# Attention tail of a two-layer encoder: masks as identity matmuls, two O/den pairs in the last units, 1/den products on GpSimd

## The chip, the cores and the metric

The kernel is one program that runs on all 8 cores of one Trainium2 chip; each core does one of the 8 sequences of the batch. The metric is the device time of the slowest core in microseconds. Most executions agree within 0.3%. Some fall in a second, slower state, in which the cores of one die (four cores) show a lower granted TensorE clock and the run is longer. "Ratio" is always the mean time of one kernel's fast runs over the mean of the other's fast runs of the same rounds, so it is not quite the ratio of the medians that are quoted beside it.

Engine names in the profile: PE is TensorE, DVE is VectorE, ACT is ScalarE, POOL is GpSimd, SP is SyncE (SPq: its queue of DMA issues).

## The reference, cut to what matters

Only layer 0's attention is touched by the change. There are 15 heads of 64 columns in three groups with dilations 1, 4 and 16, over 2048 tokens.

```python
q = rope(rms_norm(q, q_norm), pos); k = rope(rms_norm(k, k_norm), pos)
for g in range(3):                       # dilations 1, 4, 16; five heads each
    s = where(valid, q k^T * 64**-0.5, NEG_INF)      # a band of keys per query
    p = exp(s - max(s)); den = sum(p); o = (p / den) v; lse = m + log(den)
wts = softmax(stack(lses), axis=0)       # over the three groups
o = concatenate([outs[g] * wts[g]]) ; x = x + o @ w_o
# then norm, feed-forward, layer 1 (gated short convolution), feed-forward, norm
```

With those weights each group's output is its unnormalised sum of p v, divided by the sum of the three groups' denominators. The kernel uses that: it adds up the denominators of three units and multiplies each unit's output by 1/den at the end.

## The kernel before: the parts that the change and the argument touch

Attention is cut into eight units. Units 0 to 2 are the head pair (0, 1) in groups 0, 1, 2; units 3 to 5 are the pair (2, 3) in the same groups; unit 6 is head slot 4 in groups 1 and 2; unit 7 is head slot 4 in group 0. Units 6 and 7 are the tail. While TensorE does unit u, the projections of later units fill its idle time. A small scheduler orders all operations with cost estimates; each engine then runs its own queue strictly in that order.

The rotary step of a unit (`rope_a`, `rope_b`) multiplies by the cosine and sine tables, adds, and multiplies by norm factors. For that it loads a pair-swapped copy of the data ("arena<-arena" in the DMA views), stores the norm factors to DRAM ("scr<-arena"), and loads them back broadcast over the partitions ("arena<-scr").

```python
def rope_b(u, which, dst, rows=None):                      # cut
    TT("dve", rw, rw, cos_table, ALU.mult)                 # needs the projection
    TT("dve", sw, sw, sin_table, ALU.mult)                 # needs the swapped copy
    TT("dve", rw, rw, sw, ALU.add)
    TT("dve", dst, rw, rbc, ALU.mult)                      # needs the broadcast factors
# unit 7 has its queries in rows 0-63 and its keys in rows 64-127;
# after its last multiply a DMA copies the keys down ("k7")
```

Attention itself: score matmuls, one exponential on ScalarE, a 0/1 mask multiply on VectorE, output (O) and denominator (den) matmuls into one pair of banks of PSUM (the memory that matmuls write), and then an evacuation that adds the denominator into `dtot`:

```python
pO = (6, 7)                                  # the one O/den pair
bo, bd = pO
...
MMS(scores, ...)                             # one key tile after the other
ACT(P, psum, AF.Exp, scale=0.125)
TT("dve", pv, pv, map_, ALU.mult)            # the mask, 0 or 1
out_mms(P, parts)                            # O and den of one block, then evacuate(B_)

def finalize(units, lo, n):                  # 1/den, then one product per unit
    ACT(a, a, AF.Ln); ACT(a, a, AF.Exp, scale=-1.0)
    for u in units:
        TT("dve", o, o, dtot[rows, lo:lo + n], ALU.mult)   # 12 products per three units
```

## Time and profile before

The kernel before takes 1534.3 us (median of three runs, 1533.9 to 1534.9).

| stage | what the profile shows |
|---|---|
| whole span | TensorE busy 1471.2 us, 96% of 1531.6 us; the chain that ended last is 93% TensorE |
| 250 to 325 us (units 6 and 7) | the only long loose stretch; clock 0.50 from 259 to 317 us, but for one window at full clock (266 to 269 us) |
| 255 to 274 us | TensorE waits for unit 6's rotary step |

The page has a view of the span in 40 equal slices of 38.3 us. Each digit of the PE row is the busy share in tenths; each digit of the PEclk row is the granted clock in tenths. These are the two rows of the kernel before:

```profile
PE   5999997699999999999999999999999999999997
PEclk8999999589999999999999999999999999999999
```

The seventh and eighth digits of the PE row (7 and 6, 230 to 306 us) are where TensorE has less work, and the eighth and ninth of the PEclk row (5 and 8) are where its clock is halved: the tail. Apart from the start and the very end, TensorE is full everywhere else.

The timeline of one engine lists its groups of instructions. Columns: start in us, duration in us, engine, line, operation, output and input, shapes, how many; in brackets, the idle time before it and what ended that. First TensorE on core 7, the slowest core:

```profile
253.76 1.59 PE L317 MATMUL psum<-arena 128*128 128x512 bf16 x20 [2.15 <-ACT arena L511]
260.91 5.20 PE L317 MATMUL psum<-arena 128*128 128x512 bf16 x12 [5.56 <-DVE arena L333]
273.97 2.00 PE L317 MATMUL psum<-arena 64*128 64x256 bf16 x8 [7.86 <-DVE arena L333]
276.32 11.38 PE L317 MATMUL psum<-arena 64*128 64x256 bf16 x40 [0.35 <-ACT arena L328]
289.33 2.76 PE L317 MATMUL psum<-arena 128*64 128x256 bf16 x8 [1.63 <-ACT arena L343]
```

Unit 5 ends at 255.4 us. Twelve output-projection matmuls fill part of the wait; unit 6's scores (64 rows) start at 273.97. The 1.63 us at 289.33 is one wait for the single O/den pair. Then the broadcast load's issue on SyncE's queue, and VectorE on the same core:

```profile
253.07 3.14 SPq L349 DMA_DIRECT2D arena<-scr  x2
```

```profile
181.58 7.10 DVE L333 TENSOR_TENSOR arena<-arena 128x2048 bf16<-128x2048 bf16 x6 [0.88 <-DMA arena<-arena]
258.23 7.31 DVE L333 TENSOR_TENSOR arena<-arena 128x512 bf16<-128x512 bf16 x12 [0.94 <-ACT arena L328]
271.47 4.62 DVE L333 TENSOR_TENSOR arena<-arena 128x2048 bf16<-128x2048 bf16 x4 [5.92 <-DMA arena<-scr]
```

The first line is the rotary step ahead of unit 3: six multiplies in 7.10 us, 1.2 us each. The second is the twelve 1/den products of units 3 to 5, 0.6 us each, all done while the broadcast is on its way. The third is the rotary step that the tail waits for: its operand landed at 271.4 us, 18.3 us after its issue.

### The profile page before, as it was taken

Reading aid. Unit: us, or ns where it says so; the run is one execution under the profiler, and the core shown is the slowest. Engines: PE = TensorE matmul, PEld = TensorE weight load, DVE = VectorE, ACT = ScalarE, POOL = GpSimd, SP = SyncE. Lnnn points to the kernel's source line nnn. Section 1 sums busy time; section 2 is a strip of 40 time slices with the busy share of each in tenths; the row PEclk is TensorE's granted clock in tenths of the full one; section 3 lists DMA queues with packets and bytes.
Section 4 is the critical chain, followed back from the end, with each engine's and each line's share of the span. In section 5 each row is a group of like instructions: output and inputs, shape, how many; then the busy total and the mean of one; then the engine's idle time right before and its main releaser. Section 6 shows DMA issues by size and latency. Waiting matters only on the chain.

```text
span 1531.6 us, 19902 instructions; the slowest of 8 cores (1524.7 to 1531.6 us)
## 1 busy us (share of the span) xinstructions
PE 1471.2 (96%) x7312; PEld 684.8 (45%) x7312; DVE 576.6 (38%) x820; ACT 490.7 (32%) x777; POOL 380.3 (25%) x387
## 2 busy tenths in 40 slices
PE   5999997699999999999999999999999999999997
PEld 2656443243344444444444444444444444444445
DVE  4646677556114013013036444456123023032047
ACT  3566686343320220310334333333310310301333
POOL 5100000100350540630620223210530621612600
PEclk8999999589999999999999999999999999999999
DMA  9944445630330420410410433310410411312014
GB/s 252 186 86 100 86 114 110 186 76 1 55 56 1 70 42 0 83 28 2 75 22 1 62 42 49 56 28 7 76 28 3 81 28 24 60 28 49 8 55 166
DMA packets 60910, 95.00 MB, mean 62 GB/s; under 512 B 3792, under 2 KB 40912, under 8 KB 58768
## 3 DMA queue, kind: packets, MB, share of 16 engines
q0 software_dynamic: 52016, 69.18, 25.9%
q1 hardware_dynamic: 8800, 24.55, 5.2%
q8 instruction: 61, 1.00, 0.3%
q14 instruction: 33, 0.27, 0.1%
HBM read 127.37 MB, written 8.52 MB: 89 GB/s over the span
## 4 chain that ended last, share of the span: by engine, by line
PE 93%; DMA 2%; DVE 1%; ACT 1%; issue 1%; SPq 0%; POOL 0%; DVEq 0%; ACTq 0%; POOLq 0%
PE psum L317 93%; DMA arena<-scr 2%; ACT arena L328 1%; DMA arena<-xT 1%; DVE arena L336 1%; DVE arena L333 1%; ACT arena L343 0%; SPq L349 0%; DMA scr<-arena 0%; POOL arena L349 0%; DVE arena L424 0%; DVE arena L345 0%; ACT arena L423 0%; DVEq L216 0%; ACTq L216 0%
## 5 line engine op out<-in xcount | busy, mean ns | idle before, releaser
L317 PE MATMUL psum<-arena 128*128 128x512 bf16 (+5 forms) x7312 | 1471.2, 366 | 52.7 <-DVE arena L333 16.6
L317 PEld LDWEIGHTS psum<-arena 128*128 128x128 bf16 (+1 forms) x7312 | 684.8, 101 | 838.9 <-issue 136.6
L333 DVE TENSOR_TENSOR arena<-arena,psum 128x512 f32<-128x512 f32 (+1 forms) x384 | 258.2, 684 | 819.6 <-PE psum L317 811.5
L328 ACT ACTIVATE arena<-psum 128x512 bf16<-128x512 f32 (+1 forms) x306 | 201.1, 668 | 649.0 <-PE psum L317 631.3
L333 POOL TENSOR_TENSOR arena<-arena 128x512 bf16<-128x512 bf16 x288 | 304.1, 1062 | 261.6 <-ACT arena L328 165.5
L336 DVE SCALAR_TENSOR_TENSOR arena<-arena 128x512 bf16<-128x512 f32 (+2 forms) x232 | 157.8, 738 | 24.8 <-ACT arena L328 19.7
L333 DVE TENSOR_TENSOR arena<-arena 128x2048 bf16<-128x2048 bf16 (+4 forms) x146 | 125.6, 905 | 37.8 <-ACT arena L328 25.7
L423 ACT ACTIVATE arena<-arena 128x512 bf16<-128x512 f32 (+1 forms) x143 | 83.7, 607 | 132.5 <-DVE arena L333 130.2
L349 POOL DMA_DIRECT2D arena<-wdn x16 | 12.4, 778 | 430.9 <-PE psum L317 430.9
L343 ACT CAST arena<-psum 128x512 bf16<-128x512 f32 (+2 forms) x149 | 87.1, 591 | 95.2 <-PE psum L317 89.9
L328 ACT ACTIVATE arena<-arena 128x512 f32<-128x512 f32 (+2 forms) x85 | 54.3, 657 | 68.6 <-DVE arena L333 54.3
L349 POOL DMA_DIRECT2D arena<-xT x18 | 13.4, 770 | 93.0 <-DVE arena L333 73.7
L343 ACT COPY arena<-psum 128x512 f32<-128x512 f32 x38 | 22.9, 601 | 41.0 <-PE psum L317 41.0
L345 DVE CAST arena<-psum 128x512 bf16<-128x512 f32 (+2 forms) x27 | 18.4, 683 | 42.5 <-PE psum L317 42.3
L328 ACT ACTIVATE arena<-psum,arena 128x512 f32<-128x512 f32 (+1 forms) x29 | 19.5, 673 | 35.5 <-PE psum L317 35.5
L349 POOL DMA_DIRECT2D arena<-wqk x8 | 7.4, 928 | 88.4 <-PE psum L317 88.4
L349 POOL DMA_DIRECT2D arena<-wup x16 | 15.0, 937 | 43.6 <-PE psum L317 38.9
L349 POOL DMA_DIRECT2D arena<-win x8 | 7.5, 932 | 71.8 <-PE psum L317 69.1
L511 ACT ACTIVATE arena<-arena 128x1024 bf16<-128x1024 bf16 x23 | 24.1, 1057 | 2.0 <-DVE arena L345 0.7
L349 POOL DMA_DIRECT2D arena<-wo x8 | 4.4, 549 | 52.1 <-PE psum L317 52.1
L424 DVE TENSOR_TENSOR arena<-arena 128x512 bf16<-128x512 f32 (+1 forms) x17 | 11.5, 684 | 14.0 <-DMA arena<-xT 13.0
L424 POOL TENSOR_TENSOR arena<-arena 128x512 bf16<-128x512 f32 x8 | 9.3, 1173 | 19.3 <-DMA arena<-xT 19.3
(14 smaller groups left out, 26.9 us busy)
## 6 DMA issues: line engine op xcount, KB each, us to landing
arena<-wup POOLq DMA_DIRECT2D x16, 1024.0 KB, 8.4
arena<-wdn POOLq DMA_DIRECT2D x16, 1024.0 KB, 12.0
arena<-xT POOLq DMA_DIRECT2D x14, 1024.0 KB, 9.8
arena<-arena SPq DMA_DIRECT2D x14, 512.0 KB, 5.1
arena<-scr SPq DMA_DIRECT2D x14, 512.0 KB, 7.2
arena<-win POOLq DMA_DIRECT2D x8, 768.0 KB, 7.3
outT<-arena SPq DMA_DIRECT2D x24, 256.0 KB, 2.5
arena<-wqk POOLq DMA_DIRECT2D x7, 512.0 KB, 10.9
```

Of the source, the lines that this page charges most:

```text
L317: i = e.matmul(o, lhsT=l, rhs=r, start=s0, stop=s1, skip_group_check=True)
L328: return p.op("act", lambda e: e.activation(out=out, in_=in_, func=func, **kw), R, W, c_act(n, ps) + (0.09 if scale is not None and not is ...
L333: return p.op(eng, lambda e: e.tensor_tensor(out=out, in0=in0, in1=in1, op=op), R, W, cost)
L336: return p.op("dve", lambda e: e.scalar_tensor_tensor(out=out, in0=in0, scalar=scalar, in1=in1, op0=op0, op1=op1), R, W, c_dve(n, False) + ...
L343: alts.append(("act", lambda e: e.copy(out=out, in_=in_), c_act(n) + more))
L345: alts.append((e_, lambda e: e.tensor_copy(out=out, in_=in_), c_dve(n, False) + more))
L349: return p.op(eng, lambda e: e.dma_start(out=out, in_=in_), R, W, 1.3 if eng == "sp" else 1.0, chan=chan, fill=fill, nbytes=nbytes)
L423: alts = [("act", lambda e, o=o, i=xa: e.activation(out=o, in_=i, func=AF.Square), c_act(n, False)), ("dve", lambda e, o=o, i=xa: e.tensor ...
L424: ("dve", lambda e, o=o, i=xa: e.tensor_tensor(out=o, in0=i, in1=i, op=ALU.mult), c_dve(n, False))]
L511: ("act", lambda e, o=sq.ap[:, sl], i_=rw.ap[:, sl]: e.activation(out=o, in_=i_, func=AF.Square), c_act(1024, False))], None, [rw.r(*rr)], ...
```

## The change: its intent, and the diff

The intent: masks leave VectorE (a bias of -30000 is added by an identity matmul into the same PSUM group as the scores), the O/den matmuls of units 6 and 7 no longer wait for an evacuation (a second pair of banks), and the 1/den products leave VectorE (to GpSimd, low in priority). The order of the units is written as a list by head pair; that list gives the same order as before. Cut to its core:

```diff
+UNITS = [(0, 0), (1, 0), (2, 0), (0, 1), (1, 1), (2, 1)]
+FILL = "v1 p1 p2 v2 p3 p4 p5 p6 p7".split()
+FD, FP, PMU, WS = 0, 7400, 5, 0
...
-            bo, bd = pO
+            bo, bd = rings[0]
...
                     cur[:] = [B_ + 1, True]
+                    bo, bd = rings[(B_ + 1) % len(rings)]
...
+                on_pe = u >= PMU
+                if on_pe:
+                    for q in range(2):
+                        ...
+                        mms.append((PS(sb + q), ident.ap, map_, True, False))
...
-                                    kv(kb.ap[hs(h)]), qv(qb.ap[hs(h)]), True, True))
+                                    kv(kb.ap[hs(h)]), qv(qb.ap[hs(h)]), not on_pe, True))
...
+                if on_pe:
+                    ml = []
...
-                TT("dve", o, o, dtot.ap[rows, lo:lo + n], ALU.mult, [rr, dtot.r(lo, lo + n, half)], [rr], n)
+                fn = lambda e, o=o, i=dtot.ap[rows, lo:lo + n]: e.tensor_tensor(out=o, in0=o, in1=i, op=ALU.mult)
+                p.op([("dve", fn, c_dve(n, False)), ("pool", fn, 0.2 + 0.0019 * n)][1 - FD:], None,
+                     [rr, dtot.r(lo, lo + n, half)], [rr], None)
...
+            if u == PMU:
+                DMA("pool", cst.ap[:, C_MB:NCST], bias_d[:, 0:NCST - C_MB], [], [CRM], "bias", 0, ...)
+                DMA("pool", ident.ap, bias_d[:, NCST - C_MB:], [], [ident.r()], "ident", 0, 1 << 16)
...
-                attention(6, 1, [(0, 4, q_, k_)], True)
-                attention(6, 2, [(1, 4, q_, k_)], False)
+                attention(6, 1, [(0, 4, q_, k_)], True, dts[0], [pO, (0, 1)])
+                attention(6, 2, [(1, 4, q_, k_)], False, dts[0], [pO, (0, 1)])
             else:
-                attention(7, 0, [(0, 4, q_, k_)], False)
+                attention(7, 0, [(0, 4, q_, k_)], False, dts[0], [pO, (0, 1)])
```

Banks 0 and 1, the second pair, are those in which the output-projection matmuls filled the wait for unit 6. The diff also has small parts that are cut here: the second value projection gets an earlier priority, unit 7's rotary step is listed three tiles earlier, and the scheduler's cost estimate of some evacuations is lower.

## The prediction

> **What bounds the kernel.** TensorE is busy 96% of the 1531.6 us span, and the chain of waits is 93% TensorE. From 325 us until the last slice it is nearly full at clock 1.00, so only the attention tail can pay: in the stretch table, 250-325 us is the only long loose stretch (clock 0.50 from 259 to 317 us; TensorE busy 10.9, 15.1 and 17.2 of 20 us in three slices).
>
> **Why it is loose.** (1) The timeline has TensorE idle from 255.3 to 274.0 us except for 12 output-projection matmuls (260.9-266.1): unit 6's rotary step waits for the broadcast load of its norm factors, 17.7 us (about 13-18 us across cores; median of such loads 5.9 us). (2) Then units 6 and 7 run at half clock. Between blocks TensorE waits 0.9-1.6 us for its one O/den pair: about 8 us in all.
>
> **Clock.** The Trainium skill, "TensorE: Matmul & The Clock Gate", Part 1, says the clock is half or full and decided over windows of 3413 ns of activity. The trace agrees: only 0.50 and 1.00, changes at multiples of 3.41 us. Weighting each matmul by the part of the array used, I estimate from the records that windows up to about 0.68 stay at half clock and those of at least 0.69 bring back the full one. Half-array score matmuls and 64-column value matmuls reach only 0.2-0.47, so the clock stays low until output-projection matmuls (128x512) arrive near 315 us.
>
> **What the change does.**
> - Unit order is unchanged; the second value projection moves earlier. About 0.
> - 14 mask multiplies (0.69 us each) leave VectorE; TensorE does not wait for them.
> - 28 identity matmuls of 512 columns arrive on TensorE: 0.213 us each at full clock, 0.427 at half. Unit 5: +1.7 us; units 6 and 7 (20 matmuls): +8.6 us at half clock.
> - Two O/den pairs remove the block waits: -7 to -8 us.
> - The 12 output matmuls that filled the gap lose their banks to the second pair and come later: +2.6 us (full clock).
> - Unit 5 waits for a mask-bias load (224 KB) issued after unit 4's last mask; two projection tiles cover most. With the masks the broadcast starts 1-2 us later.
> - GpSimd products take about 1.17 us against 0.6 us, but inside the broadcast wait: about 0.
> - Does the clock come back earlier? A block of mask, scores and output would weigh about (0.85+0.43+1.28)/(1.8+2.8) = 0.56, below 0.69. I expect half clock through unit 6 and most of 7, and recovery later, as output matmuls come later: +4 to 5 us.
>
> Sum: +8.6+2.6+1.5+4.5-8 = about +9 us. If instead the mask matmuls do wake the clock in unit 6, it becomes 10-15 us faster; I give this one in five. Weighted: 1541 us, range 1523 to 1552. Faster over 2%: 0.02; within 2%: 0.95; slower over 2%: 0.03.
>
> **Checks.** Right: the clock still 0.50 for 50 us or more in the tail, and full clock only at output matmuls; no 1.3-1.6 us gaps between unit 6's blocks; VectorE masks gone; first unit-6 matmul 0-4 us later. Wrong: clock 1.00 before unit 7; a shorter broadcast load; new TensorE waits for GpSimd, the bias load or unit 3's denominator.
>
> **What would make it wrong.** An activity threshold below my estimate; less traffic beside the broadcast, as GpSimd issues loads behind its products; or GpSimd products holding up unit 6's first denominator evacuation.

## The result, and the profile after

After: 1551.1 us (median of four runs, 1549.7 to 1555.4). Before, in the same rounds: 1534.1 us (four runs, 1533.7 to 1534.9). The ratio is 1.0115, 95% interval 1.0095 to 1.0135. The kernel got 17 us slower, not 7.

The same two rows of the page, and the new group of GpSimd's products (busy us, then mean ns of one, then idle before):

```profile
PE   5999997699999999999999999999999999999997
PEclk8999999569999999999999999999999999999999
L751 POOL TENSOR_TENSOR arena<-arena 128x512 bf16<-128x512 bf16 (+1 forms) x32 | 46.8, 1493 | 7.2 <-ACT arena L337 7.0
```

The PE row is the same. The ninth digit of the clock row fell from 8 to 6: the clock comes back later. A product takes 1493 ns on average, although the single records show 1.15 us when nothing is beside it. The slowest core is core 5 now. Ahead of unit 3, on GpSimd, VectorE, ScalarE and TensorE of that core:

```profile
177.34 13.91 POOL L751 TENSOR_TENSOR arena<-arena 128x512 bf16<-128x512 bf16 x8 [6.99 <-ACT arena L337]
```

```profile
180.28 16.26 DVE L342 TENSOR_TENSOR arena<-arena 128x2048 bf16<-128x2048 bf16 x8
```

```profile
194.58 1.07 ACT L352 CAST arena<-psum 128x512 bf16<-128x512 f32 x2 [5.99 <-DVE arena L342]
```

```profile
195.31 14.91 PE L326 MATMUL psum<-arena 128*128 128x512 bf16 x95 [5.39 <-ACT arena L352]
```

This was full TensorE time before. Now eight rotary multiplies take 16.26 us, 2.0 us each, while the products run; TensorE stops for 5.39 us. In the single records, products that begin before the multiplies take 1.15 us and those beside them 2.14 us; the multiplies take 2.18 us beside products, 1.22 us alone. Here the two streams take turns; f1 and f2 below show another pattern.

The same stretch of the tail, again by engine: SyncE's queue, GpSimd, VectorE, TensorE:

```profile
260.51 2.91 SPq L358 DMA_DIRECT2D arena<-scr  x2
```

```profile
259.04 0.92 POOL L358 DMA_DIRECT2D arena<-wup  x1 [15.00 <-PE psum L326]
263.89 0.70 POOL L358 DMA_DIRECT2D arena<-xT  x1 [3.93 <-DVE arena L342]
264.73 17.37 POOL L751 TENSOR_TENSOR arena<-arena 128x512 bf16<-128x512 bf16 x12
```

```profile
273.22 12.23 DVE L342 TENSOR_TENSOR arena<-arena 64x2048 bf16<-64x2048 bf16 x7 [9.90 <-DMA arena<-arena]
```

```profile
260.60 1.64 PE L326 MATMUL psum<-arena 128*64 128x128 bf16 x20 [1.54 <-DVE arena L342]
285.60 6.72 PE L326 MATMUL psum<-arena 128*128 128x512 bf16 x20 [23.36 <-DVE arena L342]
```

TensorE is idle for 23.36 us. VectorE's group at 273.22 explains the end of that wait: of its seven multiplies, the first five are unit 7's, and only the last two are unit 6's. The five waited for unit 7's swapped copy, and ran at up to 2.18 us each because twelve products were running on GpSimd. The broadcast itself had landed at 278.7 us, 7 us before TensorE started.

To put a size on each part, I read the same marks on all 8 cores of each profiled run and took the mean. "Unit 6 starts" is its first score matmul (in kernels with masks on TensorE two identity matmuls come 0.9 us earlier). "Clock back" is when the records of the clock show 1.00 again in the tail.

| mean of 8 cores, us | before | after | difference |
|---|---|---|---|
| TensorE restarts at unit 3 | 191.7 | 194.8 | +3.1 |
| unit 6's broadcast issued | 252.7 | 259.6 | +6.9 |
| broadcast landed | 267.4 | 274.6 | +7.2 |
| unit 6 starts | 270.0 | 283.7 | +13.7 |
| clock back | 314.2 | 330.8 | +16.6 |
| last instruction | 1528.3 | 1545.4 | +17.1 |

So of 17.1 us: 3.1 arise up to unit 3, 3.8 more up to the broadcast's issue, 0.3 in its transfer (14.7 against 15.0 us), 6.5 between its landing and the start of unit 6 (2.6 against 9.1 us), and 3.4 from there to the end. The half-clock time between 100 and 1500 us rose from 53.8 to 72.1 us in the mean.

### The profile page after: what moved, and what is told of

Read it like the earlier page. It is cut to its first block, busy times and chain, and to the rows that moved or that the text cites. A ratio compares the mean times of both kernels' runs of the same rounds, so it can differ in the third digit from the quotient of the medians.

```text
span 1548.1 us, 19934 instructions; the slowest of 8 cores (1542.2 to 1548.1 us)
## 1 busy us (share of the span) xinstructions
PE 1483.2 (96%) x7340; PEld 686.6 (44%) x7340; DVE 563.7 (36%) x777; ACT 490.6 (32%) x772; POOL 429.8 (28%) x421
## 4 chain that ended last, share of the span: by engine, by line
PE 93%; DMA 2%; DVE 2%; issue 1%; ACT 0%; POOL 0%; DVEq 0%; SPq 0%; ACTq 0%; POOLq 0%
PE psum L326 93%; DMA arena<-xT 2%; DVE arena L342 1%; DVE arena L345 1%; DMA arena<-arena 1%; ACT arena L337 0%; POOL arena L358 0%; POOL arena L434 0%; ACT arena L352 0%; DVEq L291 0%; SPq L358 0%; DVEq L224 0%; ACT arena L433 0%; ACTq L224 0%; DVE arena L354 0%
## 5 line engine op out<-in xcount | busy, mean ns | idle before, releaser
L326 PE MATMUL psum<-arena 128*128 128x512 bf16 (+6 forms) x7340 | 1483.2, 367 | 57.2 <-DVE arena L342 25.2
L326 PEld LDWEIGHTS psum<-arena 128*128 128x128 bf16 (+2 forms) x7340 | 686.6, 101 | 853.5 <-issue 151.1
L342 DVE TENSOR_TENSOR arena<-arena 128x2048 bf16<-128x2048 bf16 (+2 forms) x98 | 106.8, 1135 | 31.5 <-ACT arena L337 16.4
L751 POOL TENSOR_TENSOR arena<-arena 128x512 bf16<-128x512 bf16 (+1 forms) x32 | 46.8, 1493 | 7.2 <-ACT arena L337 7.0
L354 DVE CAST arena<-psum 128x512 bf16<-128x512 f32 (+2 forms) x31 | 21.8, 704 | 59.2 <-PE psum L326 59.1
```

The lines of the kernel that those rows point to most:

```text
L326: i = e.matmul(o, lhsT=l, rhs=r, start=s0, stop=s1, skip_group_check=True)
L342: return p.op(eng, lambda e: e.tensor_tensor(out=out, in0=in0, in1=in1, op=op), R, W, cost)
L354: alts.append((e_, lambda e: e.tensor_copy(out=out, in_=in_), c_dve(n, False) + more))
L751: fn = lambda e, o=o, i=dtot.ap[rows, lo:lo + n]: e.tensor_tensor(out=o, in0=o, in1=i, op=ALU.mult)
```

## The experiments

The theory after reading the traces: products on GpSimd and two-input multiplies on VectorE slow each other down, and VectorE's fixed order turns that into a longer wait for unit 6. The rivals: the masks and their bias load are the cost; or the clock is; or the broadcast load.

### Parts taken back from the kernel after (first four runs)

**e1: products back on VectorE.**

```diff
-                p.op([("dve", fn, c_dve(n, False)), ("pool", fn, 0.2 + 0.0019 * n)][1 - FD:], None,
+                p.op([("dve", fn, c_dve(n, False))], None,
```

> The changed kernel with the 1/den products back on VectorE, all else kept. Theory A (GpSimd products and VectorE's rotary multiplies get in each other's way: the latter take 2.1-2.2 us instead of 1.2 while products run): rotary multiplies back to 1.2 us everywhere, the TensorE gap before unit 3 falls from 5.4 us to 1-2 us with no half-clock window there, the wait for unit 6 shortens by some 4 us although unit 7's multiplies still stand ahead of unit 6's; 1541 to 1545 us in all. Rival B (the identity matmuls at half clock cost it all): 1549 us or more.

Measured: 1543.9 us (1543.5 to 1544.6, four runs), ratio 1.0072. VectorE and TensorE of core 7 ahead of unit 3:

```profile
181.34 5.76 DVE L342 TENSOR_TENSOR arena<-arena 128x2048 bf16<-128x2048 bf16 x5
```

```profile
194.45 5.90 PE L326 MATMUL psum<-arena 128*128 128x512 bf16 x24 [3.47 <-ACT arena L352]
```

The multiplies are back at 1.2 us each. The gap shrank from 5.4 to 3.5 us and not to 1.2: the low-priority products now stand between the multiplies in VectorE's queue. The clock still fell to half there for 3.4 us on all eight cores, which the theory had excluded. About 7 us of the 17 go with the engine of the products.

**e2: products stay on GpSimd, unit 7's multiplies held behind unit 6's.**

```diff
+            after6 = [qk[0][w_].r() for w_ in range(2)] if u == 7 else []
-                   [rw.r(c0, c1, half), tabs[2 * tw].r(half=half)], ...
+                   [rw.r(c0, c1, half), tabs[2 * tw].r(half=half)] + after6, ...
```

> The changed kernel with unit 7's rotary multiplies held back until unit 6's are done (an extra read), products still on GpSimd. Theory A2 (part of unit 6's longer wait is VectorE's queue: five multiplies of unit 7, waiting for a load, stand ahead of unit 6's two): wait for unit 6 shorter by 4 to 7 us, gap before unit 3 still 5.4 us, 1544 to 1548 us. Rival (the broadcast load itself is late): wait for unit 6 unchanged at 23 us on average, 1550 us or more.

Measured: 1546.6 us (three fast runs, 1545.8 to 1547.4; one slow run at 1592.6, with which the median is 1547.0), ratio 1.0089. VectorE on core 5:

```profile
272.64 3.92 DVE L342 TENSOR_TENSOR arena<-arena 128x2048 bf16<-128x2048 bf16 x2 [9.63 <-DMA arena<-scr]
276.81 6.05 DVE L342 TENSOR_TENSOR arena<-arena 64x2048 bf16<-64x2048 bf16 x3 [0.24 <-DVE arena L342]
```

Unit 6's two multiplies now start when the broadcast lands, still at 2 us each. From landing to start of unit 6 it is 4.8 us in the mean instead of 9.1. The order alone is worth about 4 us.

**e3: masks back on VectorE** (and no bias load; the scheduler then also puts unit 6's multiplies first, so this is not the masks alone).

```diff
-FD, FP, PMU, WS = 0, 7400, 5, 0
+FD, FP, PMU, WS = 0, 7400, 8, 0
```

> The changed kernel with the masks as VectorE multiplies again (no identity matmuls, no bias load); products on GpSimd, two O/den pairs. The scheduler then also puts unit 6's rotary multiplies first. Theory (20 identity matmuls at half clock are 8 us, unit 5's 2 us, queue order 5 us): 1536 to 1542 us, gap before unit 3 still 5.4 us, half clock still until the output projection. Rival (products are all of it): 1548 us or more.

Measured: 1540.5 us (1540.1 to 1541.0, four runs), ratio 1.0050. Unit 6 starts at 272.8 us in the mean. On all eight cores TensorE then waits 7.1 to 8.7 us for the copy of unit 7's keys, as in f4 below, so the 11 us gained are a mixture.

**e4: one O/den pair again in the kernel after.**

```diff
-                attention(6, 1, [(0, 4, q_, k_)], True, dts[0], [pO, (0, 1)])
+                attention(6, 1, [(0, 4, q_, k_)], True, dts[0], [pO])
```

> The changed kernel with one O/den pair in units 6 and 7. Theory (the second pair removes 7-8 us of waits, and gives back about 3 by pushing the early output matmuls out of the gap): 1553 to 1559 us. Rival (the second pair costs more by what it pushes out of the gap than it saves): 1549 us or less.

Measured: 1555.5 us (three fast runs, 1555.1 to 1559.6; one slow run at 1765, with which the median is 1557.6), ratio 1.0155. In the kernel after, the second pair saves 4 to 6 us (4 by the medians of fast runs, 6 by the ratios); 7 to 8 were predicted.

### Parts put alone into the kernel before (next four runs)

These runs share a kernel before of 1533.2 us (median of its five fast runs, 1532.7 to 1534.5).

**f1: all products on GpSimd.**

```diff
-                TT("dve", o, o, dtot.ap[rows, lo:lo + n], ALU.mult, ...)
+                TT("pool", o, o, dtot.ap[rows, lo:lo + n], ALU.mult, ...)
```

> The kernel before with one part of the change alone: all 1/den products on GpSimd instead of VectorE. Theory (the products slow the rotary multiplies beside them): the rotary multiplies ahead of unit 3 take about 2.1 us instead of 1.2, TensorE has a gap of about 5 us ahead of unit 3 on all cores, the clock drops there; here unit 6's two final multiplies stay ahead of unit 7's, so the wait for unit 6 grows little (up to 2 us): 1536 to 1541 us. Rival (the loss needs the masks on TensorE and their bias load as well): within 1.5 us of the kernel before.

Measured: 1551.3 us (three fast runs, 1551.1 to 1552.2; one slow), ratio 1.0117. The part that looked free costs, alone, as much as the whole change. I had expected 1536 to 1541. The gap ahead of unit 3 was 5.9 us on every core, as the theory says; the wait for unit 6 grew to 19.0 us on every core (14.8 before), more than I had allowed; and after the clock had come back at 320 us it fell again for 13.7 to 17.1 us on all eight cores, which I had not foreseen: with other start times the scheduler had put other output-projection matmuls between unit 7's blocks, and their end was left with gaps of 1.5 and 0.9 us.

The longer wait for unit 6 has a cause that the theory did not foresee. VectorE and GpSimd on core 0:

```profile
273.78 9.28 DVE L333 TENSOR_TENSOR arena<-arena 128x2048 bf16<-128x2048 bf16 x1 [6.54 <-DMA arena<-scr]
```

```profile
268.54 13.43 POOL L333 TENSOR_TENSOR arena<-arena 128x512 bf16<-128x512 bf16 x12
```

The first of unit 6's two multiplies took not 2.2 but 9.28 us: it ended 1.1 us after the last of the twelve products, which ran on at 1.15 us each. On the eight cores this one multiply took 6.8 to 13.4 us. So here the streams did not take turns: VectorE was held until GpSimd's whole run of products was over. Why they alternate in the kernel after and ahead of unit 3, with instructions of the same shapes, no run shows.

**f2: only the products of units 3 to 5 on GpSimd** (five of unit 7's multiplies then stand ahead of unit 6's).

```diff
+                TT("pool" if units[0] == 3 else "dve", o, o, ...)
```

> The kernel before with only the products of units 3 to 5 on GpSimd; those of units 0 to 2 stay on VectorE. As it is scheduled, five of unit 7's rotary multiplies then stand ahead of unit 6's two final ones in VectorE's queue. Theory: no gap ahead of unit 3 (about 1 us, as before), and the loss sits in the wait for unit 6, which grows from 14.8 us to 19 to 23 us with the recovery of the clock delayed by about as much: 1538 to 1543 us. Rival (the loss is all at unit 3): within 1.5 us of the kernel before.

Measured: 1545.1 us (1544.8 to 1548.8, four runs), ratio 1.0081; 2 us above the expected range. VectorE and GpSimd on core 7:

```profile
264.21 16.52 DVE L333 TENSOR_TENSOR arena<-arena 64x2048 bf16<-64x2048 bf16 x7 [6.40 <-DMA arena<-arena]
264.21 9.41 DVE L333 TENSOR_TENSOR arena<-arena 64x2048 bf16<-64x2048 bf16 x1 [6.40 <-DMA arena<-arena]
```

```profile
259.11 13.43 POOL L333 TENSOR_TENSOR arena<-arena 128x512 bf16<-128x512 bf16 x12
```

Seven multiplies span 16.52 us. The second line is the first of the seven, alone: it took 9.41 us, held until the products were over as in f1 (9.4 to 14.7 us on the eight cores); the other six took 1.2 us each. The wait for unit 6 was 25.0 us on all cores, while the gap ahead of unit 3 stayed at 1.1 us. The clock came back no later than in the kernel before (313.9 us in the mean, against 314.2), which the theory had wrong, but then it fell again on all eight cores for 3.4 to 17.1 us. The loss of the products is thus in two places, and the tail is the larger.

**f3: identity masks and the bias load in units 5 to 7 alone.** The diff is the mask part of the change, put on the kernel before.

> The kernel before with the identity-matmul masks and the bias load in units 5 to 7 alone; products on VectorE, one O/den pair. Theory: the masks cost unit 5 about 2 us and units 6 and 7 about 8.6 us at half clock (20 matmuls of 0.427 us), and the clock recovers later by about as much; two of unit 7's multiplies ahead of unit 6's may add 2 us: 1541 to 1546 us. Rival (mask matmuls are cheap, all the loss came from the products): 1533 to 1537 us.

Measured: 1546.7 us (three fast runs, 1544.4 to 1547.8; two slow), ratio 1.0083. It is just above the range, and half for another reason than I had written. SyncE's queue and GpSimd on core 5:

```profile
253.54 0.52 SPq L350 DMA_DIRECT2D scr<-arena  x1
263.01 1.10 SPq L350 DMA_DIRECT2D arena<-scr  x2
```

```profile
252.78 0.91 POOL L350 DMA_DIRECT2D arena<-wup  x1 [15.11 <-PE psum L318]
```

The masks moved the small store of norm factors (16 KB) to just behind the issue of a 1 MB weight load. In the kernel before, the store comes 1.2 us ahead of that load, lands in 1.7 us, and the broadcast is issued 2.6 us after the store; here the store took 6.6 to 9.5 us to land and the broadcast was issued 7.8 us after it in the mean. A delay of 3 us became one of 9. No run holds the load in this kernel, so that reading rests on the trace.

**f4: two O/den pairs alone.**

```diff
-            bo, bd = pO
+            bo, bd = rings[0]
-                attention(6, 1, [(0, 4, q_, k_)], True)
+                attention(6, 1, [(0, 4, q_, k_)], True, [pO, (0, 1)])
```

> The kernel before with two O/den pairs in units 6 and 7 alone. Theory: the block waits of 0.9 to 1.6 us go away (6 to 8 us), but the 12 output-projection matmuls that filled the wait for unit 6 have lost their banks and come later (2.6 us at full clock), so 1528 to 1533 us, with the clock back a few us earlier. Rival (what the pair gains is given back through the clock and the later output matmuls): 1534 to 1540 us.

Measured: 1537.6 us (three fast runs, 1536.8 to 1540.0; one slow, with which the median is 1538.8), ratio 1.0023 (0.9999 to 1.0048). The rival's number came true, for a reason that neither had named. TensorE on core 0:

```profile
275.26 24.42 PE L317 MATMUL psum<-arena 64*128 64x256 bf16 x88 [0.34 <-ACT arena L328]
307.70 1.86 PE L317 MATMUL psum<-arena 64*128 64x256 bf16 x8 [8.02 <-DMA arena<-arena]
```

Unit 6 runs without waits between blocks and ends early. Then TensorE waits 8.02 us for the copy of unit 7's keys. VectorE did unit 7's multiplies between unit 6's evacuations, so the copy was issued at 299.8 us, against 291.5 us on that core before. The gain was there, and was spent one step later.

### What follows from these, tested (last six runs)

**g1: two pairs, and unit 7's rotary step right behind unit 6's.** To the edit of f4 comes e2's and this:

```diff
-                p.pri = 1000 * u + 300 if u else -150
+                p.pri = 5995 if u == 7 else 1000 * u + 300 if u else -150
```

> The kernel before with two O/den pairs in units 6 and 7, and unit 7's rotary steps right behind unit 6's in VectorE's queue, so that the copy of unit 7's keys starts early. The two pairs alone came out at 1538.8 us with an 8.0 us wait of TensorE for that copy. Theory (the pairs do save the block waits, but VectorE's order gave it back as that wait): the 8 us wait is gone, the block waits too, and the time is 1526 to 1531 us, below the kernel before. Rival (the pairs lose because the 12 output-projection matmuls come later and the clock stays half for longer): 1534 to 1539 us.

Measured: 1532.6 us (three fast runs, 1531.8 to 1533.9; one slow), ratio 0.9993. Of the kernel before only fast runs count in this row (1533.8 to 1535.7). The 8 us wait is gone:

```profile
288.82 41.39 PE L317 MATMUL psum<-arena 128*64 128x128 bf16 x163 [1.84 <-DVE arena L333]
```

On core 0 the score matmuls of unit 7 are inside this unbroken group. In the mean the clock came back at 308.7 us, 5.6 us earlier than before, but the last instruction came only 2.8 us earlier: the 12 output-projection matmuls that had filled the wait for unit 6 now come later, about 2.6 us of work at full clock (12 times 0.213 us). By the slowest core nearly nothing is left. So the theory was right on the wait and its range was missed; the rival's range (1534 to 1539) was missed as well, from below.

**g2: as g1, and the 1 MB weight load held until unit 6's rotary step is done.**

```diff
-            return load_w(slots[i], dview, kc, cols_, "w%d" % i), slots[i]
+            return load_w(slots[i], dview, kc, cols_, "w%d" % i, [qk[0][1].r()] if wk["n"] == 1 else []), slots[i]
```

> As the run of two pairs with unit 7 early, and with the first load of feed-forward weights (1 MB, issued about when the broadcast load is) held until unit 6's rotary step is done. Theory (the broadcast of norm factors takes 11 to 18 us because that load shares its engines): the broadcast lands in 6 to 9 us, unit 6 starts 3 to 8 us earlier than in the run without the hold, and the time falls by 2 to 6 us more. Rival (the broadcast's length is its own): landing and time unchanged within 1.5 us.

Measured: four fast runs, 1537.6, 1538.2, 1539.1 and 1558.3 us, and two slow ones; ratio 1.0059, interval 0.9991 to 1.0127. That is not faster than g1. The first half of the theory held: the broadcast landed 7.7 us after its issue instead of 14.5. The edit was faulty, though: the memory that the hold names is later used for other data, and the load was issued for real only at 374 us. GpSimd, and TensorE, on core 5:

```profile
373.83 0.88 POOL L349 DMA_DIRECT2D arena<-wup  x1 [60.16 <-DVE arena L333]
```

```profile
389.88 9.81 PE L317 MATMUL psum<-arena 128*128 128x512 bf16 x32 [9.99 <-DMA arena<-wup]
```

The feed-forward layer waited 9.99 us for its weights. h1 mends this.

**g3: the kernel before, TensorE kept busy with 60 dummy matmuls while it waits for unit 6.**

```diff
+        def keep_busy(n):
+            MMS([(PS(6), onesN, h_ap(0, 0, 512), True, True)] * n, ...)
             elif u == 6:
+                p.pri = 5500
+                keep_busy(60)
+                p.pri = 6000
```

> The kernel before with 60 dummy matmuls of 512 columns (12.8 us at full clock) put on TensorE while it waits for unit 6; nothing else is changed, and the dummies' sums are overwritten. Theory (units 6 and 7 are slow because the idle wait drops the clock[...]): the clock stays 1.00 at the start of unit 6, half clock in the tail falls from 54 us to below 35 us, and the time falls by 4 to 12 us, to 1522 to 1530 us. Rival (the half clock costs little, as TensorE waits for other engines there anyhow): half clock falls, the time stays within 2 us of the kernel before or rises by the dummies' overrun.

Measured: 1534.4 us (1533.9 to 1534.9, four runs), ratio 1.0001. The half-clock time of the program fell from 53.8 to 40.1 us in the mean, and unit 6 began at full clock on every core. It fell to half at 275 us on cores 5 and 7, within 3 us, and at 280 to 284 us on the other six. The dummies made unit 6 start 2.9 us later, and from there to the clock's return it took 43.3 us instead of 44.2. The rival holds for this stretch: the first 8 to 9 us of unit 6 at full clock, on those six cores, were worth about 1 us. TensorE waits for exponentials and evacuations there (on core 2, for example, 1.53 us twice for an evacuation by ScalarE), so I take the slower clock to fill idle time mostly; that reading is argued. What the half clock costs in the rest of the tail is not shown by this run.

**h1: as g1, with the hold placed so that the load goes out right behind unit 6's rotary step.**

```diff
                 if u == 7:
+                    first_w = load_w(slots[0], wup_d[0][:, 0:512], 8, 512, "w0", [qk[0][1].r()])
                     load_x(1)
```

> As the run of two pairs with unit 7 early, with the first feed-forward weight load held behind unit 6's rotary step, this time so that it is issued right after it; in the last try the hold sat on memory that later data takes over, the load went out at 374 us and TensorE waited 10 us for it. Theory: the broadcast lands about 8 us after its issue, unit 6 starts 12.6 us after unit 5 on every core, the wait for the weights is gone: 1520 to 1528 us, faster than the kernel before and the one after. Rival (the freed engines only move the contention to the next loads): 1530 to 1536 us.

Measured: 1526.7 us (four fast runs, 1525.9 to 1529.5; one slow), ratio 0.9957, interval 0.9943 to 0.9971. This beats the kernel before by about 7 us and the one after by 24. TensorE, SyncE's queue and GpSimd on core 7:

```profile
255.56 1.59 PE L317 MATMUL psum<-arena 128*128 128x512 bf16 x20 [2.16 <-ACT arena L511]
269.76 2.00 PE L317 MATMUL psum<-arena 64*128 64x256 bf16 x8 [12.61 <-DVE arena L333]
```

```profile
254.87 1.16 SPq L349 DMA_DIRECT2D arena<-scr  x2
```

```profile
270.94 0.91 POOL L349 DMA_DIRECT2D arena<-wup  x1
```

Unit 6 starts 12.6 us after unit 5's end on every core; in the kernel before this was 13.1 to 18.6 us. The broadcast landed 7.4 us after its issue in the mean, at 262.2 on this core. The rest of the wait is now VectorE's products, which stand ahead of unit 6's multiplies.

**h2: the kernel after, with only that hold.**

```diff
                 if u == 7:
+                    first_w = load_w(slots[0], wup_d[0][:, 0:512], 8, 512, "w0", [qk[0][1].r()])
```

> The kernel after with only that weight load held until unit 6's rotary step is done; products stay on GpSimd, and four of unit 7's multiplies stay ahead of unit 6's. Theory (part of the longer wait for unit 6 is the load: the broadcast took about 18 us to land): the swap and broadcast loads land within 10 us, the wait for unit 6 falls from 23.4 to 15 to 20 us, and the time from 1551 to 1541 to 1548 us. Rival (VectorE's slow multiplies alone set the start of unit 6): within 2 us of 1551.

Measured: 1540.8 us (three fast runs, 1538.7 to 1542.7; one slow), ratio 1.0052, against 1.0115 for the kernel after. VectorE and TensorE on core 5:

```profile
262.21 13.99 DVE L342 TENSOR_TENSOR arena<-arena 128x2048 bf16<-128x2048 bf16 x8
277.51 1.91 DVE L342 TENSOR_TENSOR arena<-arena 128x2048 bf16<-128x2048 bf16 x1 [1.32 <-DMA arena<-scr]
```

```profile
274.24 15.95 PE L326 MATMUL psum<-arena 128*128 128x512 bf16 x49 [11.90 <-DVE arena L342]
```

The multiplies are still slow (13.99 us for eight), but they start at once at 262.2, because unit 7's swapped copy no longer shares the DMA engines with the weights; the wait for unit 6, from unit 5's last matmul to unit 6's first score matmul, is 13.0 us in the mean, not 22.4. (The 23.4 us in the expectation is 1 us too long by this reading.) Nine microseconds go away although the products, the masks and their costs are all still there. The hold saved the kernel with two pairs only 2.0 us by the mean of the cores (g1 to h1, last instruction 1525.5 to 1523.5; 6 us by the medians of the slowest core), and the kernel after 9.5 us. So the weight load is not what the change added, as the broadcast beside it took 15 us before too; but slow multiplies behind a late load cost far more than the late load alone.

**h3: the kernel after with both repairs of e1 and e2.** The diffs are those.

> The kernel after with both repairs: products back on VectorE, and unit 7's rotary multiplies behind unit 6's. Alone they gave 1543.9 and 1547.0 us. Theory (both act on the wait for unit 6, so they overlap): unit 6's wait is 14 to 17 us as in the kernel before, and 1539 to 1543 us, so that 6 to 9 us of loss remain, which are the masks' and their bias load's. Rival (the gains add): 1537 to 1539.9 us.

Measured: fast runs 1543.9 and 1544.0 us, two of four slow; ratio 1.0066. This is 1 us outside what the theory expected and well outside the rival. The two repairs do not add: with the products on VectorE, the order is worth nothing (e1: 1543.9 us). The mean wait for unit 6 is 16.6 us and differs between cores (13.3 to 14.1 us on four, 18.0 to 20.7 us on the other four), with the landing of the broadcast, 11.5 to 18.9 us after its issue.

## Why the prediction was right or wrong, point by point

- **The direction and the class** were right: slower, within 2%. The size was wrong: +17 us for +7, and the measured median lies inside the range of 1523 to 1552 only at its very edge.
- **The step that failed: "GpSimd products take about 1.17 us against 0.6 us, but inside the broadcast wait: about 0."** The duration alone is right (1.15 us; the 1.17 is the cost estimate in the diff, 0.2 + 0.0019 x 512). What is wrong is "about 0". First, this counted the products of units 3 to 5 only; those of units 0 to 2 run beside the rotary step ahead of unit 3, in time that was full on TensorE: +3.1 us there (1.3 us of it stays when the products go back to VectorE at low priority, e1). Second, the products are not alone in the broadcast wait: VectorE's multiplies run there, and take up to 2.18 us instead of 1.22 us. Third, as the scheduler arranged VectorE's queue, five of unit 7's multiplies stand ahead of unit 6's two (in f1, with the same products on GpSimd, they do not; there one of unit 6's own multiplies was held for 6.8 to 13.4 us). The term measured: from broadcast landing to unit 6's start 9.1 us instead of 2.6. Taking the products back gives 7 us (e1); putting them alone into the kernel before costs 18 us (f1).
- The Trainium skill states this conflict on "SBUF — State Buffer", section "Who interferes with whom": a VectorE instruction with two SBUF inputs contends with a GpSimd instruction that reads SBUF. Its section "Summary: rules for kernel authors" adds that the second of the two to issue blocks until the first is done. The kernel after agrees: 1.15 us alone and 2.14 us together for the product, 1.22 us and 2.18 us for the multiply. In the tails of f1 and f2 the measurement differs: one multiply was blocked over several products, not one, for 6.8 to 14.7 us. I had not looked for it, as my prediction asked what a product costs and not what it does to its neighbours.
- **"First unit-6 matmul 0-4 us later"**: 13.7 us later by the score matmuls. This check showed the failure at once, and the new wait was for VectorE, which was not in my list of things to look for.
- **"With the masks the broadcast starts 1-2 us later"**, with +1.5 us for unit 5: it was issued 6.9 us later, of which 3.1 were there at unit 3 already. With the masks on VectorE 2.7 us less arises between the two (e3: broadcast issued at 256.4, unit 3 at 194.4 us). That includes the bias load; the runs do not divide it further. Another part of the 3.8 us may be the clock, which is at half for 3.4 to 6.8 us after the new gap on all eight cores (before: on one core); that is argued from the records, not tested.
- **Masks at half clock, +8.6 us; output matmuls moved, +2.6; clock later, +4.5; block waits, -8**: together +7.7 us. From the start of unit 6 to the end the measured difference is +3.4 us. The block waits did go (e4: 4 to 6 us, and no waits of 1.3 to 1.6 us between blocks in the trace after) and the clock did stay at half for 61 to 68 us, coming back only at output-projection matmuls. So this group of terms was too large by 4.3 us in sum; that this offset part of the other error was luck. The whole account: the sum of +9.2 us was short by 3.1 us at unit 3, 2.3 us from there to the broadcast's issue (3.8 for 1.5), and 6.8 us in the wait for unit 6 (0.3 + 6.5), and too long by 4.3 us here, which gives 17.1. g3 agrees with that: full clock in the first part of unit 6 was worth 1 us only.
- **The threshold of about 0.69 for the clock's return** was too sharp. I redid the estimate: the part of a 3.41 us window in which columns stream, times the part of the array in use. In the kernel before, the largest window that stayed at half clock has 0.66 (core 7, at 34 us) and the smallest that brought the full clock back 0.68 (core 4, at 261 us; some matmul records of this core are missing). In other runs the two overlap: windows of 0.72 (g3, core 1, at 309 us) and 0.74 (f1, core 3, at 337 us) did not bring it back, and windows of 0.68 (g1, cores 3 and 6, at 302 and 306 us) did. For the fall there is no limit either: a window of 0.37 was followed by half clock (g3, core 1, at 190 us), and windows of 0.30 were not (g1, cores 0, 1 and 7, at 304 to 317 us).
- **The masks alone** cost 13 us on the kernel before (f3) and 11 us when taken back (e3, with the shifts named there); their matmuls were put at 10.3 us (1.7 + 8.6). In f3 the larger part is a later start of unit 6 (279.0 us in the mean against 270.0): a small store that landed late, behind a large load.
- The parts alone add up to 18 + 13 + 4 = 35 us on the kernel before, and the whole change costs 17. They all act on one wait, and each lets the scheduler arrange the tail anew. No division of the 17 us by part is thus unique; the division by place in the table above is. What stays open is how much time the half clock costs after the first 9 us of the tail, what the masks cost without the shifts that they cause, what the small parts of the diff do (no run takes back all three large parts), and when VectorE is held for a whole run of products and when not.

## What to carry to other kernels

An operation that is moved to an idle engine is free only if it also leaves the shared paths of the engine that it helps: look at what runs beside it, in every place where it runs, and compare the neighbours' durations before and after. In a queue with fixed order, freeing an engine lets other work in ahead of the one that somebody waits for; name that one and hold the others behind it. When a wait ends on a small load or store, look for the large transfer issued beside it, and issue that one a few microseconds later: this was worth 2 to 6 us in the kernel with two pairs (g1 to h1) and 10 us in the kernel after (h2).

## What the Trainium skill lacked or had wrong

- "SBUF — State Buffer", section "Who interferes with whom": right on which pairs conflict. It lacks what two steady streams do to each other. In the kernel after they alternate and both slow down: 1.15 to 2.14 us for the GpSimd product, 1.22 to 2.18 us for the VectorE multiply. In the tails of f1 and f2 they do not: one multiply was blocked for 6.8 to 14.7 us, until the last product was done, while the products kept their 1.15 us. It also lacks how a profile shows this: the blocked time is counted as busy time of the instruction (9.28 us for one multiply in f1) and not as a wait.
- "TensorE: Matmul & The Clock Gate", Part 1: the two clock values and the window of 3413 ns agree with the records (only 0.50 and 1.00, changes at multiples of 3.41 us). It names no share of busyness at which a window counts. The runs give no clean limit for it: by array-weighted share, as I estimate it, a window of 0.68 brought the full clock back (g1) and one of 0.74 did not (f1).
- "DMA: Bandwidth & Descriptors", section "Issuing engines are not separate DMA queues", says that transfers from several engines interleave on the same 16 DMA engines. The runs agree: 14.7 us for a broadcast beside a 1 MB load that another engine issued, 7.4 us without it (kernel before and h1). The page lacks a duration for a small transfer with a large one just ahead of it: a 16 KB store landed in 1.7 us when it went first (kernel before), and in 6.6 to 9.5 us when the 1 MB load was issued 0.8 us earlier (f3).
